# A quarter of the later weight splits made by GpSimd, and a planner with new prices

## The chip, the cores and the metric

The kernel runs on one core of a Trainium2 chip. The metric is the device time of one execution in microseconds, lower is better. A measured time is the median over runs; a profiled execution is one more run, with the hardware profiler on.

## The reference

One decoder layer on 512 tokens of width 2048, batch 1, in float32:

```python
mod = silu(c) @ w_ada + b_ada                  # six vectors of 2048: sh1 sc1 g1 sh2 sc2 g2
h   = rms_norm(x, norm1_g) * (1 + sc1) + sh1
u   = h @ w_in                                 # columns: conv b, c, h | q | 3 branches of k, v | gates
y_conv = u_b * causal_conv3(u_c * u_h)
k_cmp, v_cmp = compress(k), compress(v)        # gelu MLP over 31 overlapping blocks of 32 tokens
y_attn = g0 * compressed + g1 * selected + g2 * window attention   # 8 heads of 128, 2 kv heads
x   = x + g1 * ([rms_norm(y_conv) | rms_norm(y_attn)] @ w_out)
h   = rms_norm(x, norm2_g) * (1 + sc2) + sh2
x   = x + g2 * (relu(h @ w_ff1) ** 2 @ w_ff2)  # inner width 8192
out = rms_norm(x, normf_g)
```

## The kernel before, in words

**Precision.** Every large product of float32 matrices is made of three matmuls in the type fp32r. Each operand is split into a high part (ScalarE copies it into fp32r) and a low part (the operand minus its high part, a subtraction on VectorE). `mm3` issues high by high, high by low and low by high into one PSUM bank. So each block of weights needs a DMA, a copy on ScalarE and a subtraction on VectorE before its last third of matmuls can run.

**`weights(src)`** does that for the blocks of the layer's first part: 128 x 1024 (or 128 x 1072) float32, a DMA on the SP queue into a ring of three (`wraw`, tile `raw`), the ScalarE copy into `wh`, the VectorE subtraction into `wl`. `wh` and `wl` lie side by side in one tile, which the profile calls `wh` for both; there are two such tiles (`whl`), so a block's copy waits until the block two before it has been used up. Blocks of the compression weights take other buffers (tile `sw`, `spare=True`). `weights` is called 122 times: 16 `w_kv` and 16 `w_cv` blocks alternate in six stretches, then 32 of `w_conv` with 16 compression blocks between them, 8 of `w_v`, 16 of `w_q`, 16 of `w_oc` and 2 of `w_oa`. A block of the first two kinds is used by 24 matmuls of 512 columns.

**Other work on VectorE.** The conditioning `mod` is 192 dot products of a 128 x 1024 block of `w_ada` with `cs` (a `scalar_tensor_tensor` with an accumulator, tile `t<-wa,cs` in the profile), spread over the first part as a filler; 128 of them (`todo`) aren't needed until the attention. Rotary embeddings (`rope`, tile `rt`), the convolution (`vz`, `y`), the compression inputs (`ct`, `chi`, `clo`) and the softmax work run on VectorE too.

**Stages.** The first planned part (projections, convolution, compression) ends near 560 us of the profile. The second, attention with the out-projection of the convolution half (`out_conv`, tile `pw`) between its steps, ends near 747 us. The third holds the rest of the out-projection and the feed-forward part; it has its own splits (`hilo`, tile `hl`), which the change doesn't touch.

**The order of the work.** Nothing runs in the order of the Python text. An `Order` object stands in for the engines: it records each call with a cost (`price`, in us) and a lag, and `emit` makes a list schedule from them (`plan`) and issues the instructions in its order. The order on each engine is then fixed; on the chip the engines only wait for each other. The three planned parts have an `Order` each. The first two plan six times and keep the plan with the shortest planned time; the third plans once. Among the works that could begin at the same time, an engine takes the one with the earliest latest start (`late`), which is worked out backwards from planned TensorE times. GpSimd issues no instruction in the first two planned parts; in the third it issues DMAs.

Of the kernel before, what the change touches and what calls it, by code (L numbers as in the profile page):

```python
# [9 lines left out]
F32 = mybir.dt.float32  # L10
# [3 lines left out]
OP = mybir.AluOpType  # L14
AX = mybir.AxisListType

P = 128
# [18 lines left out]
NMAIN = 29  # L36
# [13 lines left out]
class Order:  # L50
# [8 lines left out]
        __slots__ = ("i", "eng", "call", "cost", "lag", "size", "preds", "succs", "late", "loose", "born",  # L59
                     "begin", "ready", "left", "lane", "slack", "due")  # L60

    def __init__(self, tc, tag, count, passes=1):
        self.tc, self.tag, self.count, self.passes = tc, tag, count, passes
        self.lane, self.kept, self.slack, self.wide = 0, set(), 0.0, (0.11, 0.00182)
        self.nodes, self.past, self.seen, self.rings = [], {}, {}, {}
        self.outer, self.loose, self.due = set(), False, 0.0
        for e in ("tensor", "vector", "scalar", "sync", "gpsimd"):
            setattr(self, e, Order.Engine(self, e, getattr(tc.nc, e)))
# [25 lines left out]
    def price(self, eng, op, out, ins, kw):  # L94

        n = Order.width(out)
        if "dma" in op:
            return (0.42 if eng == "sync" else 0.55), 0.0
        if eng == "tensor":
            if op == "matmul" and ins[0].dtype == F32:  # L100
                return max(self.wide[0], n * self.wide[1]), 0.2
            return (0.109 if op == "transpose" else max(0.1, 0.0015 + n * 0.000453)), 0.2
        if eng == "scalar":
            aps = len(ins) - 1
            more = 0.1 if kw.get("accum_out") is not None else 0.0
            return (0.18 if n < 16 else 0.09 + 0.00084 * n + (0.09 * max(0, aps) if not more else 0.19)), 0.16
        if op == "tensor_reduce":
            rows = max(Order.width(x) for x in ins)
            return 0.068 + 0.00104 * rows * (1.7 if n > 16 else 1), 0.14
        if n < 16:  # L110
            return 0.1, 0.14
        if op == "scalar_tensor_tensor":
            return 0.14 + 0.00101 * n, 0.14
        if op in ("tensor_scalar", "tensor_copy", "memset"):
            return 0.13 + 0.0005 * n, 0.14
        return 0.068 + 0.00104 * n, 0.14

    def record(self, eng, op, real, args, kw):
        is_ap = lambda x: hasattr(x, "dep_tracking_offset")
# [158 lines left out]
def hybrid_layer(ctx: ExitStack, tc: tile.TileContext, a, out):  # L278
    nc = tc.nc
# [10 lines left out]
    def slot(dtype=F32, name="m"):  # L290
        return mainp.tile([P, SLOT], dtype, name=name, tag="m")

    def pair(dtype=F32, name="m"):
        return slot(dtype, name)[:, :2 * T].rearrange("p (a b) -> p a b", a=2)
# [22 lines left out]
        tc.keep_in_program_order(filler(nc.tensor))  # L317

    xs = [pair(name="x2") for _ in range(NK // 2)]
    nc = order = Order(tc, xs[0].tensor.tag, NMAIN, passes=6)  # L320
    order.wide = (0.24, 0.0021)
    ts = [small.tile([P, T], F32, name="t", tag="t", bufs=5) for _ in range(5)]
    scr, temps = ts[0].bitcast(BF16), cycle(ts[1:])
# [18 lines left out]
    class lane:  # L342

        def __init__(self, n):
            self.n = n
# [15 lines left out]
    class floating:  # L361
# [4 lines left out]
        def __exit__(self, *_):  # L366
            order.loose = False

    def weights(src, cols=1024, spare=False):
        raw = next(wraw)[:, :cols]  # L370
        nc.sync.dma_start(out=raw, in_=src)
        wh, wl = (slot(F32R, name="sw") for _ in range(2)) if spare else next(whl)
        wh, wl = wh[:, :cols], wl[:, :cols]
        nc.scalar.activation(wh, raw, AF.Copy)
        nc.vector.tensor_tensor(out=wl, in0=raw, in1=wh.bitcast(F32), op=OP.subtract)
        return wh, wl

    def split(dst, src):
# [241 lines left out]
    def blob(s):  # L620
        return weights(a[steps[s][0]][steps[s][1]])
# [14 lines left out]
    for c in ada_steps(M_SH1 * NK):  # L636
        pass
    w = weights(a["w_kv"][0])
    low(*tokens(0, spread_r))
    order.slack = 1.0  # L640
# [8 lines left out]
    for s, (name, k) in enumerate(steps[:-1]):  # L649
# [4 lines left out]
        wh, wl = w  # L654
# [78 lines left out]
    def project(src, tiles):  # L733
        ps = bank()
        for half in range(2):
            wh, wl = ahead.pop() if ahead else weights(src(half))
            for j in range(8):
                k = half * 8 + j
                s = slice(j * P, (j + 1) * P)
                mm3(ps, wh[:, s], wl[:, s], tiles[k][:, 0], tiles[k][:, 1], k == 0, k == NK - 1)  # L740
            tick()
            more_ada(1)
        return ps
# [78 lines left out]
    for j in range(8):  # L822
# [4 lines left out]
        for i in range(3):  # L827
            n = 3 * j + i
# [30 lines left out]
    for g in range(NG):  # L859
        pv = [bank() for _ in range(NQ)]  # L860
        for blk in range(4):
            wh, wl = weights(a["w_v"][g * 4 + blk], BLOB)
# [11 lines left out]
        for t in range(NQ):  # L874
            if t % 2 == 0:
# [4 lines left out]
                                    in1=vv[g, t][:, 0].bitcast(F32), op=OP.subtract)  # L880
# [31 lines left out]
    for g in range(NG):  # L912
        pq = [bank() for _ in range(NR)]
        order_k = range(NK) if g < NG - 1 else range(NK - 1, -1, -1)
        for at, k in enumerate(order_k):
            if at % 2 == 0:
                wh, wl = weights(a["w_q"][g * 8 + k // 2])
# [32 lines left out]
    x1 = []  # L950
    nc = tc.nc
    temps = cycle(ts)
    nc = order = Order(tc, mix[0].tensor.tag, NMAIN, passes=6)
# [145 lines left out]
    front.close()  # L1099


    nc = order = Order(tc, x1[0].tensor.tag, NMAIN)
    ffn = ExitStack()
    ffp = ffn.enter_context(tc.tile_pool(name="ffp", bufs=2, reuse_waits="tile"))
    psf = ffn.enter_context(tc.tile_pool(name="psf", bufs=8, space=PSUM, reuse_waits="tile"))
# [32 lines left out]
    def raw_blob(src):  # L1138
        raw = next(rw)
        nc.sync.dma_start(out=raw, in_=src)  # L1140
        return raw

    def hl_tile(moved=False):
        t, o = next(hl), place[0] * SHIFT
        return t[:, o:o + 1024], Low(t, 1024 + o, moved)

    def hilo(dst, src, minus=False):
        high, low = dst
        nc.scalar.activation(high, src, AF.Copy, scale=-1.0 if minus else 1.0)
        for c in low.parts() if isinstance(low, Low) else [slice(0, 1024)]:  # L1150
            x, h = src[:, c], high[:, c].bitcast(F32)
            if minus:
                nc.vector.scalar_tensor_tensor(out=low[:, c], in0=x, scalar=-1.0, in1=h,
                                               op0=OP.mult, op1=OP.subtract)
            else:
                nc.vector.tensor_tensor(out=low[:, c], in0=x, in1=h, op=OP.subtract)
        return dst
# [20 lines left out]
    for k in range(8):  # L1178
        wh, wl = oa[k] if k < 2 else hilo(hl_tile(), raw_blob(a["w_oa"][k]))
# [254 lines left out]
    x1 = []  # L1434
# [60 lines left out]
    for f in range(8):  # L1495
# [7 lines left out]
        for q in range(3 if last else 4):  # L1503
            raw = [raw_blob(a["w_f2"][4 * f + q, b]) for b in range(4)]
# [127 lines left out]
```

## Time and profile before

| | |
|---|---|
| median of 3 runs | 2099.41 us (2098.15 to 2101.2) |
| profiled execution, its own time | 2105.6 us |
| its span, first to last instruction | 2103.8 us |
| mean granted TensorE clock | 0.989 |
| PE busy | 2060.6 us (98%), 15006 matmuls |
| DVE (VectorE) busy | 1886.2 us (90%) |
| ACT (ScalarE) busy | 1009.8 us (48%) |
| POOL (GpSimd) busy | 128.2 us (6%) |
| read from and written to HBM | 383.53 MB, 68.16 MB |

Nearly all instructions carry one source line, that of the planner's call, so work is told apart by its tiles: `ps` and `pw` are PSUM tiles of the first two parts, `pf` those of the third; `wh<-raw` is a copy into a high part, `wh<-raw,wh` the subtraction into a low one. Rows of a timeline begin with the start and the duration in us; brackets hold the idle time in front of the instruction on its engine and what ended it.

### The profile page before, as it was taken

The numbers are of one execution on the slowest core, as the hardware profiler recorded it, in microseconds if no ns is written. First come the engines' busy times: TensorE is split into PE (matmuls) and PEld (weight loads), VectorE is DVE, ScalarE is ACT, GpSimd is POOL, SyncE is SP. The second block draws the span as 40 slices with busy tenths as digits, with TensorE's granted clock in tenths as the row PEclk, the third lists the DMA queues.
The fourth block names the chain that finished last, engine by engine and source line by source line (L and its number), as shares of the span: only waits on it lengthen the run. The fifth ranks groups of instructions, "written<-read, shape, count | busy, mean of one in ns | idle before, by whom it ended". The sixth has DMA issues, their size and how long they took to land.

```text
span 2103.8 us, 38070 instructions
## 1 busy us (share of the span) xinstructions
PE 2060.6 (98%) x15006; PEld 1918.9 (91%) x15006; DVE 1886.2 (90%) x3104; ACT 1009.8 (48%) x1469; POOL 128.2 (6%) x244
## 2 busy tenths in 40 slices
PE   8999999999999999999999999999999999999997
PEld 6888787898888779999999999999999999999996
DVE  7998987887998647999999999999899999999997
ACT  5432333232455435766666666666433333333354
POOL 0000000000000001021122112211000000000000
PEclk8999999999999999999999999999999999999998
DMA  8996488888521244376676667669876466466442
GB/s 331 342 341 246 160 299 320 310 306 293 187 91 41 71 140 161 121 236 211 205 217 202 204 205 219 205 203 305 302 277 220 150 244 240 144 235 247 153 163 90
DMA packets 144274, 454.17 MB, mean 216 GB/s; under 512 B 15840, under 2 KB 20320, under 8 KB 144096
## 3 DMA queue, kind: packets, MB, share of 16 engines
q1 hardware_dynamic: 108960, 386.72, 52.8%
q0 software_dynamic: 34048, 63.98, 9.7%
q8 instruction: 118, 1.93, 0.4%
q10 hardware_dynamic: 1088, 1.05, 0.1%
q14 instruction: 60, 0.49, 0.1%
HBM read 383.53 MB, written 68.16 MB: 215 GB/s over the span
## 4 chain that ended last, share of the span: by engine, by line
PE 76%; DVE 7%; DMA 3%; ACT 2%; issue 1%; DVEq 0%; ACTq 0%; SPq 0%
PE pf L124 56%; PE ps L124 11%; PE pw L124 4%; PE pv L124 2%; PE s L124 2%; DVE t L124 1%; DVE hl L124 1%; PE pt L124 1%; DVE x L124 1%; DMA raw<-in_cmp_w 1%; DMA rw<-in_w_f 1%; DMA wa<-in_w_ada 1%; DMA tk<-g 1%; DVE tk L124 1%; DVE wh L124 1%
## 5 line engine op out<-in xcount | busy, mean ns | idle before, releaser
L124 PE MATMUL pf<-tk,hl 128*128 128x256 f32 x10704 | 1222.7, 277 | 3.4 <-DVE hl L124 3.1
L124 PEld LDWEIGHTS pf<-tk,hl 128*128 128x128 f32 x10704 | 1220.3, 188 | 4.7 <-DVE hl L124 3.5
L124 ACT ACTIVATE hl<-rw 128x1024 fp32r<-128x1024 f32 x269 | 285.6, 1062 | 332.6 <-PE pf L124 287.1
L124 DVE TENSOR_TENSOR hl<-rw,hl 128x1024 fp32r<-128x1024 f32 (+2 forms) x351 | 336.0, 967 | 30.7 <-ACT hl L124 30.5
L124 ACT ACTIVATE hl<-sg 128x1024 fp32r<-128x1024 f32 x180 | 191.2, 1063 | 221.9 <-PE pf L124 175.0
L124 DVE SCALAR_TENSOR_TENSOR t<-wa,cs 128x1024 bf16<-128x1024 f32 x192 | 234.2, 1220 | 25.4 <-DMA wa<-in_w_ada 23.1
L124 PE MATMUL ps<-h_m,wh 128*128 128x512 f32 x1080 | 252.4, 390 | 1.2 <-DVE wh L124 0.8
L124 PEld LDWEIGHTS ps<-h_m,wh 128*128 128x128 f32 x1080 | 201.1, 188 | 43.0 <-DVE wh L124 1.2
L124 ACT ACTIVATE wh<-raw 128x1024 fp32r<-128x1024 f32 (+1 forms) x106 | 112.6, 1062 | 251.1 <-PE ps L124 221.1
L124 DVE TENSOR_TENSOR hl<-sg,hl 128x1024 fp32r<-128x1024 f32 (+2 forms) x193 | 187.9, 985 | 28.1 <-ACT hl L124 28.1
L124 PE MATMUL ps<-h,wh 128*128 128x512 f32 x840 | 201.0, 395 | 3.7 <-ACT h L124 2.3
L124 PEld LDWEIGHTS ps<-h,wh 128*128 128x128 f32 x840 | 159.1, 191 | 38.4 <-ACT h L124 2.7
L124 DVE TENSOR_TENSOR sg<-sg,rw 128x1024 f32<-128x1024 f32 x120 | 145.9, 1216 | 0.2
L124 DVE SCALAR_TENSOR_TENSOR x<-pf,mod,x 128x256 f32<-128x256 f32 (+1 forms) x280 | 132.0, 484 | 15.6 <-PE pf L124 13.6
L124 DVE TENSOR_TENSOR wh<-raw,wh 128x1024 fp32r<-128x1024 f32 (+1 forms) x106 | 129.6, 1223 | 18.1 <-ACT wh L124 17.6
L124 POOL DMA_DIRECT2D g<-gt x192 | 101.2, 532 | 377.3 <-ACT hl L124 255.1
L124 PE MATMUL pw<-mix,wh 128*128 128x512 f32 x384 | 110.3, 409 | 0.0
L124 ACT ACTIVATE t<-t 128x512 f32<-128x512 f32 (+3 forms) x131 | 74.8, 571 | 18.6 <-DVE t L124 16.4
L124 DVE TENSOR_TENSOR sg<-rw 128x1024 f32<-128x1024 f32 x60 | 73.1, 1218 | 11.4 <-DMA rw<-in_w_f 6.7
L124 PEld LDWEIGHTS pw<-mix,wh 128*128 128x128 f32 x384 | 69.7, 192 | 11.1 <-issue 0.7
L124 DVE TENSOR_TENSOR rw<-rw 128x1024 f32<-128x1024 f32 x60 | 72.9, 1215 | 0.0
L124 ACT ACTIVATE gt<-t 128x512 fp32r<-128x512 f32 x96 | 60.4, 630 | 17.1 <-DVE t L124 13.9
(213 smaller groups left out, 1770.3 us busy)
## 6 DMA issues: line engine op xcount, KB each, us to landing
rw<-in_w_f SPq DMA_DIRECT2D x263, 512.0 KB, 4.0
wa<-in_w_ada SPq DMA_DIRECT2D x192, 512.0 KB, 6.2
tk<-g SPq DMA_DIRECT2D x114, 512.0 KB, 6.2
g<-gt POOLq DMA_DIRECT2D x192, 256.0 KB, 4.1
raw<-in_w_conv SPq DMA_DIRECT2D x32, 512.0 KB, 4.2
x<-in_xt SPq DMA_DIRECT2D x16, 512.0 KB, 6.9
raw<-in_w_kv SPq DMA_DIRECT2D x16, 512.0 KB, 4.7
raw<-in_w_cv SPq DMA_DIRECT2D x16, 512.0 KB, 4.1
```

The lines of the kernel that those rows point to most:

```text
L124: x.i, x.eng, x.call = len(self.nodes), eng, (lambda: real(*args, **kw))
```

## The change

```diff
+    def __init__(self, tc, tag, count, passes=1, pace=0.000456):
 ...
     if eng == "tensor":
         ...
-        return (0.109 if op == "transpose" else max(0.1, 0.0015 + n * 0.000453)), 0.2
+        return (0.109 if op == "transpose" else max(0.1, n * self.pace)), 0.2
+    if eng == "gpsimd":
+        return 0.3 + 0.0021 * n, 0.2
 ...
     if n < 16:
-        return 0.1, 0.14
+        return 0.12, 0.14
     if op == "scalar_tensor_tensor":
-        return 0.14 + 0.00101 * n, 0.14
+        return 0.14 + 0.00101 * n + (0.07 if kw.get("accum_out") is not None else 0.0), 0.14
 ...
-    return 0.068 + 0.00104 * n, 0.14
+    return 0.068 + 0.00104 * n + (0.1 if op == "tensor_tensor_reduce" or out.shape[0] < P else 0.0), 0.14
 ...
-nc = order = Order(tc, xs[0].tensor.tag, NMAIN, passes=6)        # first part
+nc = order = Order(tc, xs[0].tensor.tag, NMAIN, passes=6, pace=0.000444)
 ...
+    blobs = [0]
     def weights(src, cols=1024, spare=False):
         ...
         nc.scalar.activation(wh, raw, AF.Copy)
-        nc.vector.tensor_tensor(out=wl, in0=raw, in1=wh.bitcast(F32), op=OP.subtract)
+        blobs[0] += 1
+        engine = nc.gpsimd if blobs[0] > 16 and blobs[0] % 4 == 0 else nc.vector
+        engine.tensor_tensor(out=wl, in0=raw, in1=wh.bitcast(F32), op=OP.subtract)
 ...
-nc = order = Order(tc, x1[0].tensor.tag, NMAIN)                  # third part
+nc = order = Order(tc, x1[0].tensor.tag, NMAIN, pace=0.000444)
```

Of the 122 blocks that `weights` makes, those with the numbers 20, 24, 28 and so on to 120 get their low half from GpSimd: 26 blocks. The compression's blocks have odd numbers from 39 to 73, so none of these is among them. The copies on ScalarE and the matmuls stay.

The planner's prices change in all three parts: a matmul of 512 columns goes from 0.2335 to 0.2273 us in the first and third part (0.2335 in the second), one of 256 columns from 0.1175 to 0.1137 us. On VectorE, operations on fewer than 16 elements, `scalar_tensor_tensor` with an accumulator, `tensor_tensor_reduce`, and operations on fewer than 128 partitions are priced higher. A GpSimd operation on 1024 elements is priced at 2.45 us. The orders on all engines are planned anew with these.

More of the change, by code (lines that the diff above doesn't have):

```diff
@@ L60 @@
                      "begin", "ready", "left", "lane", "slack", "due")
-    def __init__(self, tc, tag, count, passes=1):
+    def __init__(self, tc, tag, count, passes=1, pace=0.000456):
         self.tc, self.tag, self.count, self.passes = tc, tag, count, passes
-        self.lane, self.kept, self.slack, self.wide = 0, set(), 0.0, (0.11, 0.00182)
+        self.lane, self.kept, self.slack, self.wide, self.pace = 0, set(), 0.0, (0.11, 0.00182), pace
         self.nodes, self.past, self.seen, self.rings = [], {}, {}, {}
```

## The prediction

> **What bounds the kernel now.** I read the page first: the shares.
>
> ```profile
> span 2103.8 us, 38070 instructions
> PE 2060.6 (98%) x15006; PEld 1918.9 (91%) x15006; DVE 1886.2 (90%) x3104; ACT 1009.8 (48%) x1469; POOL 128.2 (6%) x244
> ```
>
> TensorE is busy 98% of the span, so an engine that is relieved helps only where TensorE waits for it. Busy time also hides a halved clock, so I next cut the span into stretches. The columns are the length, busy time and instruction count of PE, PEld, DVE, ACT and POOL, then the granted TensorE clock, DMA share and GB/s.
>
> ```profile
> 60.00:160.00 100.00, 100.00 (x443) 82.84 (x442) 98.36 (x179) 39.68 (x51) 0.00 (x0) 1.00 0.92 345
> 176.00:226.00 50.00, 49.38 (x216) 39.92 (x215) 46.31 (x69) 13.56 (x16) 0.00 (x0) 1.00 0.46 160
> 226.00:237.00 11.00, 6.71 (x29) 4.60 (x27) 11.00 (x15) 6.07 (x8) 0.00 (x0) 0.96 0.28 95
> 237.00:244.00 7.00, 7.00 (x24) 6.06 (x25) 6.93 (x10) 1.44 (x2) 0.00 (x0) 0.57 0.58 192
> 244.00:440.00 196.00, 193.84 (x1001) 161.44 (x1001) 163.91 (x241) 63.41 (x76) 0.00 (x0) 1.00 0.83 301
> 440.00:549.00 109.00, 108.47 (x592) 94.94 (x591) 90.64 (x146) 34.37 (x53) 0.00 (x0) 1.00 0.78 283
> 549.00:562.00 13.00, 11.51 (x57) 9.36 (x55) 12.39 (x26) 3.60 (x6) 0.00 (x0) 1.00 0.72 250
> 562.00:572.00 10.00, 9.94 (x42) 8.44 (x43) 7.48 (x36) 5.07 (x20) 0.00 (x0) 0.66 0.42 150
> 572.00:730.00 158.00, 158.00 (x832) 126.53 (x831) 129.91 (x373) 86.35 (x219) 0.00 (x0) 1.00 0.18 61
> 900.00:1450.00 550.00, 550.00 (x4847) 550.00 (x4846) 520.44 (x747) 355.49 (x497) 108.83 (x207) 1.00 0.69 212
> 1500.00:1520.00 20.00, 17.27 (x134) 16.88 (x133) 16.96 (x30) 6.01 (x8) 2.63 (x5) 0.91 0.96 316
> 1530.00:2050.00 520.00, 520.00 (x4583) 520.00 (x4582) 500.88 (x740) 209.96 (x209) 0.58 (x2) 1.00 0.59 207
> ```
>
> From 60 to 160 us VectorE is 98% busy and TensorE still never waits: 443 matmuls of 512 columns in 100 us, 0.2257 us each. The feed-forward stretches run at 550/4847 = 0.1135 us per matmul of 256 columns. There nothing is to be gained. What VectorE can give back lies in two places. From 226 to 237 us VectorE is busy all 11.0 us and TensorE idles 11.0 - 6.71 = 4.3 us; the clock is then 0.57 for 7 us, another 7 x 0.43 = 3.0 us. At the seam to the attention, 549 to 562 us, it idles 1.5 us and then runs at 0.66 for 10 us, 3.4 us more. Which waits these are, the order in time shows (start, length, and in brackets the idle time before and who ended it):
>
> ```profile
> 227.63 4.19 PE L124 MATMUL ps<-h_m,wh 128*128 128x512 f32 x17 [0.82 <-DVE wh L124]
> 232.39 0.33 PE L124 MATMUL ps<-sw,chi 128*66 128x256 f32 x1 [0.57 <-ACT sw L124]
> 236.97 0.48 PE L124 MATMUL ps<-sw,chi 128*66 128x256 f32 x1 [2.89 <-DVE sw L124]
> 220.44 1.06 ACT L124 ACTIVATE wh<-raw 128x1024 fp32r<-128x1024 f32 x1 [0.15 <-ACT vz L124]
> 226.37 1.21 DVE L124 TENSOR_TENSOR wh<-raw,wh 128x1024 fp32r<-128x1024 f32 x1
> 231.30 1.04 ACT L124 ACTIVATE sw<-raw 128x1024 fp32r<-128x1024 f32 x1
> 235.71 1.21 DVE L124 TENSOR_TENSOR sw<-raw,sw 128x1024 fp32r<-128x1024 f32 x1
> ```
>
> The two VectorE waits, 0.82 and 2.89 us, are subtractions that stood in VectorE's queue: the `wh` one could have begun at 221.5 and began at 226.37, the `sw` one could at 232.3 and began at 235.71.
>
> **The change part by part.** *Blocks off VectorE.* The durations per piece:
>
> ```profile
> L124 DVE TENSOR_TENSOR wh<-raw,wh 128x1024 fp32r<-128x1024 f32 (+1 forms) x106 | 129.6, 1223 | 18.1 <-ACT wh L124 17.6
> L124 ACT ACTIVATE wh<-raw 128x1024 fp32r<-128x1024 f32 (+1 forms) x106 | 112.6, 1062 | 251.1 <-PE ps L124 221.1 <-issue 13.0 <-PE pw L124 7.0
> ```
>
> 26 x 1.223 = 31.8 us leave VectorE. Counting the `wh<-raw,wh` subtractions in order of time and skipping the compression's numbers, block 28 is the one at 177.8, 32 at 202.4, and 36 is the row at 226.37 above. So three lie in the full stretch before the long wait, 3 x 1.21 = 3.6 us, against 2.89 us of wait for `sw`; and block 36 itself is the 0.82 us wait. GpSimd has nothing else up to 730 us (POOL 0.00 in every row).
>
> *What GpSimd costs.* No GpSimd arithmetic is in this trace. The nearest row is VectorE's own 1.22 us, the lower end; the upper end that matters is where TensorE would notice: a block's 24 matmuls take 24 x 0.2257 = 5.4 us, the copy takes 1.06 of them, so 4.3 us. I take the planner's price from the diff, 2.45 us, near the middle. Then copy and subtraction are 3.5 of 5.4 us: the matmuls of the block before hide it, and the cost is nothing for 25 blocks. Block 36 would be ready at 221.5 + 2.45 = 224.0, before the 226.4 at which VectorE now begins it. The Trainium skill, GPSIMD Reference, section Elementwise — side-by-side cycle accounting, gives 4497 ns for 2048 elements of this operation, from which 2.25 us is an estimate for 1024; no run here shows it yet, and the sum would stay the same.
>
> (a) So of 0.82 + 2.89 + 3.0 = 6.7 us nearly all could go. But the next compression block is behind a transfer:
>
> ```profile
> 243.41 1.06 ACT L124 ACTIVATE sw<-raw 128x1024 fp32r<-128x1024 f32 x1 [5.56 <-DMA raw<-in_cmp_w]
> ```
>
> A TensorE that is earlier meets that one earlier. I take -5.0; ends -6.7 and +2.
>
> (b) Seam. Four blocks of `w_q` (92 to 104) leave VectorE, 4.9 us, but its last dot product waited for its transfer, and TensorE's wait was for what comes behind it:
>
> ```profile
> 559.20 1.23 DVE L124 SCALAR_TENSOR_TENSOR t<-wa,cs 128x1024 bf16<-128x1024 f32 x1 [0.40 <-DMA wa<-in_w_ada]
> 561.98 0.56 PE L124 MATMUL s<-kslc,q 128*128 128x160 f32 x3 [1.49 <-DVE pc L124]
> ```
>
> I take -1.0; ends -4.9 (wait and slow clock gone) and +1.
>
> (c) Block 120 lies where the attention ends, on the chain that set the end:
>
> ```profile
> 734.42 1.06 ACT L124 ACTIVATE wh<-raw 128x1024 fp32r<-128x1024 f32 x1 [0.79 <-PE pw L124]
> 735.51 1.23 DVE L124 TENSOR_TENSOR wh<-raw,wh 128x1024 fp32r<-128x1024 f32 x1
> 736.66 5.38 DVE L124 SCALAR_TENSOR_TENSOR ya<-ya,vec,sacc 128x512 f32<-128x512 f32 x8
> 735.96 0.60 ACT L124 ACTIVATE sacc<-pt 128x512 f32<-128x512 f32 x1 [0.48 <-PE pt L124]
> 749.36 10.73 PE L124 MATMUL pf<-mixa,wh 128*128 128x512 f32 x46 [1.00 <-DVE wh L124]
> ```
>
> VectorE gains nothing: `ya` needs `sacc`, which ends at 736.56 anyway. TensorE gets its low half at 735.5 + 2.45 = 737.9 instead of 736.7, 1.2 us later, with little else to do. I take +1.0; ends 0 and +1.3. Block 116 and the two before it sit amid attention work that fills TensorE (158.00 of 158.00 us).
>
> (d) *Prices.* The old plan has matmuls of 512 columns at 0.2335 us, the chip 0.2257, the new plan 0.2273; for 256 columns 0.1175, 0.1135, 0.1137. VectorE was too cheap:
>
> ```profile
> L124 DVE SCALAR_TENSOR_TENSOR t<-wa,cs 128x1024 bf16<-128x1024 f32 x192 | 234.2, 1220 | 25.4 <-DMA wa<-in_w_ada 23.1
> L124 DVE TENSOR_TENSOR rt<-part,rot 64x512 f32<-64x512 f32 (+1 forms) x18 | 11.8, 684 | 0.2
> ```
>
> The dots go from 1.174 to 1.244 (chip 1.220), the half-height rotary steps from 0.600 to 0.700 (chip 0.684). The old plan thus had TensorE 3% late and VectorE early, which is how (a) could go unseen in it; its repair is counted there. No instruction is added. But all orders are redrawn. From 244 to 549 us TensorE idles only 2.2 + 0.5 = 2.7 us; a redrawn order can lose there as well as win: +0.5, ends -2.7 and +4. In the feed-forward the one stretch with a loss is 1500 to 1520 us, 2.7 us idle and 20 x 0.09 = 1.8 us of clock: 0, ends -3 and +3.
>
> Sum: -5.0 - 1.0 + 1.0 + 0.5 = -4.5 us. Each duration is from the profiled execution, 2105.6 us (span 2103.8 and 1.8 around it), 6.2 us over the median of the runs; I set the difference against the median: 2099.4 - 4.5 = 2094.9 us.
>
> **The rivals.** *The stall only moves.* The first wait shrinks, but the transfer for the next compression block (the row at 243.41) or the redrawn order puts another in its place, and a gap of a few us anywhere brings the slow clock back, as behind both waits above. Then (a) is worth 2 instead of 5: 2099.4 - 2.0 - 1.0 + 1.0 + 0.5 = 2097.9 us. For it speaks that the 5.56 us of that row are a transfer, which no engine's relief shortens; against it, that its buffer is freed by the engines that now run earlier.
>
> *VectorE is held while GpSimd reads (slower).* If an instruction of VectorE with two inputs in SBUF cannot run beside one of GpSimd, each block costs VectorE up to 2.45 us of standing still for 1.22 saved, a net +1.2. It decides as soon as VectorE is held more than 1.2 us per block. Between 176 and 226 us VectorE has 3.7 us idle, enough for block 28; blocks 32 and 36 add 2.5 us ahead of `sw`, so that (a) turns into about +2 (2.5 more, 0.8 less, and the slow clock stays). The 17 blocks from 244 to 549 us add 17 x 1.2 = 21 us to VectorE, which has 196.0 - 163.9 + 109.0 - 90.6 = 50 us idle there; at 0.2 us each on TensorE, +3.5. At block 120 `ya` starts at 737.9 in place of 736.7: +1.3 more. Together 2.0 + 3.5 + 1.0 + 1.3 = +7.8: 2107.2 us. Nearly all VectorE work in that stretch (dots, subtractions) has two SBUF inputs, which speaks for its size; that no GpSimd arithmetic is in the trace leaves it open. The Trainium skill states this rule, in SBUF — State Buffer, section Who interferes with whom: a VectorE instruction with two SBUF inputs and a GpSimd instruction that reads SBUF exclude each other, and the second to issue blocks until the first is done. By that rule the sum would be the +7.8 just worked out; no row here can show it, since POOL computes nothing in these stretches.
>
> *GpSimd is slower than 4.3 us.* Then TensorE waits in 22 blocks; at 5 us it would be 22 x 0.7 = 15 us: 2110 us. Nothing in the trace speaks for it; it counts with the slower cases.
>
> **How the numbers follow.** About 0.2%, 4.2 us, is what a measurement can tell from no change: the borders are 2095.2 and 2103.6. The forecast's case, 0.42, with a range of its own from 2088 to 2095; the stall that moves, with small net changes of both signs, 0.35; slower, 0.23 (held 0.2, slow GpSimd 0.03). The held case does not get more, since part of VectorE's standing still falls into its idle time. Low end of the range: (a) -6.7, (b) -4.9 and (c) 0 give 2087.8, so 2087. High end: the held case, 2107. That leaves about 0.2 outside.
>
> **What would show it.** Right: 26 subtractions on POOL of about 2.5 us, VectorE's count of `wh<-raw,wh` down to 80, the wait for `sw` near 230 us under 1 us and no stretch at half clock behind it. Held: VectorE's subtractions and dots beside a POOL instruction take 2 to 3.5 us instead of 1.22. Moved: the same idle sum of TensorE before 560 us under other names. Wrong altogether: the feed-forward, planned once with new prices, changes by more than 3 us; there (e.g. at 1500 us) I count nothing.

## The result, and the profile after

The changed kernel takes 2114.8 us (median of 6 runs, 2113.6 to 2122.4), the one before 2099.4 in the same session: a ratio of 1.0083, 95% interval 1.0067 to 1.0099. It is slower by 15 us by the medians and 17 by the ratio, where 2094.9 us was forecast and the range ended at 2107. The ratios here and below are those on record with their intervals, and differ somewhat from the quotients of the medians (here 1.0073); the median given with each is its own.

The page of the changed kernel, shares:

```profile
span 2113.7 us, 38138 instructions
PE 2057.6 (97%) x15006; PEld 1919.3 (91%) x15006; DVE 1891.1 (89%) x3078; ACT 1007.7 (48%) x1469; POOL 195.7 (9%) x270
```

VectorE has 26 instructions fewer (3078 against 3104), which took 31.8 us, and yet 1891.1 us of busy time in place of 1886.2. So the others grew by 36.7 us (1891.1 less 1886.2 - 31.8). The groups show GpSimd's work, and dot products that were 1220 ns each and are now 1268 in the mean, with 41.8 us of idle time in front of them instead of 25.4:

```profile
L126 POOL TENSOR_TENSOR wh<-raw,wh 128x1024 fp32r<-128x1024 f32 (+1 forms) x26 | 67.5, 2597 | 686.3 <-ACT wh L126 458.1 <-DVE aff L126 131.0 <-PE pw L126 49.1
L126 DVE SCALAR_TENSOR_TENSOR t<-wa,cs 128x1024 bf16<-128x1024 f32 x192 | 243.4, 1268 | 41.8 <-DMA wa<-in_w_ada 39.8
```

Where the time of VectorE went is seen beside each GpSimd subtraction. In order of time, three of them with VectorE's instructions next to them (start, length):

```profile
131.40 3.41 POOL L126 TENSOR_TENSOR wh<-raw,wh 128x1024 fp32r<-128x1024 f32 x1 [130.96 <-DVE aff L126]
131.33 1.22 DVE L126 SCALAR_TENSOR_TENSOR t<-wa,cs 128x1024 bf16<-128x1024 f32 x1
132.49 2.34 DVE L126 SCALAR_TENSOR_TENSOR mod<-acc,vec 128x1 f32<-128x1 f32 x1
...
310.76 3.26 POOL L126 TENSOR_TENSOR wh<-raw,wh 128x1024 fp32r<-128x1024 f32 x1 [18.63 <-ACT wh L126]
311.69 2.87 DVE L126 TENSOR_TENSOR sacc<-sacc,t 128x512 f32<-128x512 f32 x1
...
657.95 2.40 POOL L126 TENSOR_TENSOR wh<-raw,wh 128x1024 fp32r<-128x1024 f32 x1 [48.11 <-PE pt L126]
658.27 0.28 DVE L126 CUSTOM_DVE_ANT_0 p<-s,causal 128x128 f32<-128x128 f32 x1
658.86 0.69 DVE L126 TENSOR_TENSOR tt<-pt,tt 128x512 fp32r<-128x512 f32 x1 [0.30 <-ACT tt L126]
```

No row names the hold as a wait; it is read from the lengths. At 131.4 GpSimd's row begins, 3.41 us long where an undisturbed one takes 2.40, so it first waits for the dot product that VectorE is in, until about 132.5. Then it runs, and VectorE's next instruction, one element wide, stands until 134.8, when GpSimd is done. `sacc<-sacc,t`, 0.68 us before, takes 2.87 and ends 0.5 us behind GpSimd. At 658 VectorE reads its first operand from PSUM, and nothing is held: 0.28 and 0.69 us are these groups' usual times. The instructions beside all 26 subtractions are together 35.0 us longer than instructions of the same kind and shape are without GpSimd (in `e3`): 10.6 us beside the first five, 21.5 beside the 17 from block 40 to 104, 2.8 beside the four in the attention. Each block saves VectorE 1.22 us, so the first five cost it 4.5 us net and the 17 only 0.8.

What TensorE makes of it (the two long waits, then stretches with the columns as before):

```profile
235.28 0.48 PE L126 MATMUL ps<-sw,chi 128*66 128x256 f32 x1 [5.64 <-ACT sw L126]
576.24 0.93 PE L126 MATMUL s<-kslc,q 128*128 128x160 f32 x3 [9.00 <-DVE pc L126]
```

```profile
226.00:240.00 14.00, 8.36 (x31) 6.53 (x30) 14.00 (x19) 7.45 (x9) 0.00 (x0) 0.78 0.23 67
240.00:440.00 200.00, 192.20 (x978) 159.77 (x977) 161.15 (x222) 63.06 (x75) 28.68 (x11) 1.00 0.81 290
564.00:576.00 12.00, 2.48 (x15) 1.66 (x13) 9.96 (x23) 1.07 (x2) 0.00 (x0) 0.68 0.80 273
576.00:586.00 10.00, 9.76 (x38) 9.00 (x39) 5.41 (x36) 5.25 (x20) 0.00 (x0) 0.53 0.24 95
```

The wait near 230 us did not shrink, it grew from 4.3 us of idle time in all to 5.6. It carries another name now, ScalarE's `sw`, but it is still VectorE's queue: ScalarE makes `sw` behind its copy into `chi`, and that one stood for VectorE's `ct`.

```profile
233.22 1.06 ACT L126 ACTIVATE chi<-ct 128x1024 fp32r<-128x1024 f32 x1 [3.62 <-DVE ct L126]
```

From 240 to 440 us TensorE idles 7.8 us, where it was 2.2 in 244 to 440. The seam to the attention, 1.5 us before, is 9.5 us idle in one stretch, with the clock at 0.53 for 10 us behind it. The last dot product, behind which the attention's first work stands, starts at 573.5 instead of 559.2 (rows of the dots, shortest, median and longest in ns, then first and last start, before and after):

```profile
L124 DVE SCALAR_TENSOR_TENSOR t<-wa,cs x192: 1161/1219/1243, 16.6 to 559.2; 128x1024 bf16<-128x1024 f32 x192
```

```profile
L126 DVE SCALAR_TENSOR_TENSOR t<-wa,cs x192: 1202/1220/3302, 16.3 to 573.5; 128x1024 bf16<-128x1024 f32 x192
```

The third part got shorter. From its first matmul to the end, before and after; and the stretch that had the one loss before:

```profile
747.70:2103.80 1356.10, 1333.25 (x11448) 1320.94 (x11448) 1242.20 (x1890) 711.54 (x960) 128.02 (x240) 0.99 0.62 205
```

```profile
765.00:2113.70 1348.70, 1330.12 (x11448) 1319.04 (x11448) 1241.88 (x1890) 709.08 (x960) 127.92 (x240) 1.00 0.63 207
1500.00:1520.00 20.00, 19.76 (x173) 19.55 (x172) 18.81 (x30) 8.87 (x12) 0.00 (x0) 1.00 0.80 296
```

So the loss of the first two parts is about 17 us in these two profiles, and 7.4 us came back in the third.

### The profile page after: what moved, and what is told of

Same layout as the page of the kernel before. It is cut to its first block, busy times and chain, and to the rows that moved or that the text cites. A ratio compares the mean times of both kernels' runs of the same rounds, so it can differ in the third digit from the quotient of the medians.

```text
span 2113.7 us, 38138 instructions
## 1 busy us (share of the span) xinstructions
PE 2057.6 (97%) x15006; PEld 1919.3 (91%) x15006; DVE 1891.1 (89%) x3078; ACT 1007.7 (48%) x1469; POOL 195.7 (9%) x270
## 4 chain that ended last, share of the span: by engine, by line
PE 85%; DVE 8%; DMA 4%; issue 2%; ACT 1%; SPq 0%; DVEq 0%; ACTq 0%
PE pf L126 61%; PE ps L126 16%; PE pw L126 4%; DMA wa<-in_w_ada 2%; DVE t L126 2%; PE pv L126 2%; PE s L126 2%; DVE wh L126 1%; PE pt L126 1%; DVE rt L126 1%; DMA raw<-in_cmp_w 1%; DMA tk<-g 1%; DMA rw<-in_w_f 1%; DVE x L126 0%; DVE vz L126 0%
## 5 line engine op out<-in xcount | busy, mean ns | idle before, releaser
L126 DVE SCALAR_TENSOR_TENSOR t<-wa,cs 128x1024 bf16<-128x1024 f32 x192 | 243.4, 1268 | 41.8 <-DMA wa<-in_w_ada 39.8
L126 POOL TENSOR_TENSOR wh<-raw,wh 128x1024 fp32r<-128x1024 f32 (+1 forms) x26 | 67.5, 2597 | 686.3 <-ACT wh L126 458.1
L126 DVE TENSOR_TENSOR wh<-raw,wh 128x1024 fp32r<-128x1024 f32 (+1 forms) x80 | 97.9, 1224 | 12.4 <-ACT wh L126 11.8
L126 DVE TENSOR_TENSOR sg<-rw 128x1024 f32<-128x1024 f32 x60 | 73.1, 1218 | 11.4 <-DMA rw<-in_w_f 9.2
```

The source lines that it names most:

```text
L126: x.i, x.eng, x.call = len(self.nodes), eng, (lambda: real(*args, **kw))
```

## The experiments

The theories: **H**, VectorE is held while GpSimd reads, and that costs the time; **P**, the new prices draw worse orders; **L**, GpSimd's low half comes later than VectorE's; and on how a hold reaches TensorE, **D** (through the late dot products at the seam) and **Q** (through waits before it). All ratios are to the kernel before; edits are shown shortened. A new order of the instructions is drawn for every version, and the first two parts keep the old one only in `e3`.

**1. New prices alone.** `e1_prices_only`:

```diff
-engine = nc.gpsimd if blobs[0] > 16 and blobs[0] % 4 == 0 else nc.vector
+engine = nc.vector
```

> All new prices, but VectorE makes every low half, as before the change. Theory H (held): VectorE instructions with two SBUF inputs stand still while GpSimd reads, at moments the plan does not know of, and that is what costs TensorE the time before the third part; then without GpSimd the third part begins near 748 us as before (746 to 751) and the total is the changed kernel's third part on top of it, 2092 to 2097 us. Theory P (prices): the new prices by themselves draw a worse order for the first two parts, and holding costs only the net 35.0 - 31.8 = 3 us of VectorE; then the third part begins at 760 us or later and the total is 2109 to 2114 us.

Measured: 0.9998 (0.9982 to 1.0015), median 2100.3 us. Neither: the 15 us are gone without GpSimd, but the third part's gain is not visible in the sum either, so the new prices by themselves cost the first two parts about what they bring the third. Its third part begins at 746.6 us, as theory H had it, but the total is above H's range. The profile shows both sides. From 226 to 240 us TensorE idles only 1.6 us at full clock, so the new order does repair the stall that the prediction put under (a). At the seam, with no GpSimd at all, TensorE arrives at 548.5 us, ten earlier than before, and waits 11.65 us, longer than in the changed kernel.

```profile
226.00:240.00 14.00, 12.39 (x61) 10.01 (x60) 13.97 (x19) 6.83 (x10) 0.00 (x0) 1.00 0.33 105
563.02 0.93 PE L126 MATMUL s<-kslc,q 128*128 128x160 f32 x3 [11.65 <-DVE pc L126]
```

**2. GpSimd alone.** `e2_gpsimd_old_prices` keeps the 26 subtractions and GpSimd's price; every other price is the old one:

```diff
-nc = order = Order(..., passes=6, pace=0.000444)    # and likewise in the other two parts
+nc = order = Order(..., passes=6, pace=0.000444, new=False)
```

> The 26 low halves on GpSimd, at the planner's 2.45 us each, but all other prices as before the change, in all three parts. Theory H: the first two parts lose as in the changed kernel, the third gains nothing: 2112 to 2124 us, with VectorE instructions stretched by 30 to 40 us in sum. Theory P: about the net 3 us of VectorE: 2099 to 2104 us.

Measured: 1.0106 (1.0082 to 1.0130), 2121.7 us. Theory H: GpSimd costs 22 us by itself (17 to 27 by the interval), the order drawn anew for it included. VectorE has 26 instructions fewer, and is busy 1892.9 us in this profile, 38.5 more than 1886.2 - 31.8. TensorE doesn't wait at the seam here: its last work ahead of it ends at 574.4 us, and the last dot product starts at 572.8. The loss is in waits ahead of it.

**3. New prices in the third part alone.** `e3_third_part`: no GpSimd, `new=False` in the first two parts, so their orders are those of the kernel before.

> No GpSimd; the first two parts keep the old prices, the third part alone is planned with the new ones. If the third part's 7 us (1348.6 us in the changed kernel, 1356.1 before) are the new prices' doing, this gives 2099.4 - 7 = 2092 us (2089 to 2095) under both theories. If they come from how the third part is entered, it stays at 2099 (2096 to 2102).

Measured: 0.9964 (0.9951 to 0.9978), 2092.0 us. The 7.6 us are the new prices' doing in the third part. This version beats both kernels. Its third part:

```profile
737.60:2084.70 1347.10, 1328.39 (x11448) 1317.50 (x11448) 1241.80 (x1890) 709.46 (x960) 127.89 (x240) 1.00 0.62 207
```

It also warns about single profiles: the first two parts, in the same order, end at 737.6 us here and at 747.7 in the profile before. Most of that is the slow clock: here TensorE waits 2.85 us for the same `sw` subtraction and 0.86 at the seam (at 555.0), and neither stretch behind is slow.

```profile
234.54 0.33 PE L126 MATMUL ps<-sw,chi 128*66 128x256 f32 x1 [2.85 <-DVE sw L126]
237.00:244.00 7.00, 6.36 (x29) 4.96 (x28) 6.90 (x12) 2.30 (x3) 0.00 (x0) 1.00 0.48 160
552.00:562.00 10.00, 9.10 (x57) 7.38 (x56) 9.58 (x45) 5.91 (x20) 0.00 (x0) 1.00 0.60 221
```

So single differences under 10 us between profiles, those of the section above too, say where time went and not how much the change costs; that is read from the medians and ratios.

**4. A plan that knows of the hold.** `e4_plan_knows`, in `plan`:

```diff
+if e == "gpsimd" and not x.size: at = max(at, free["vector"])
 ...
 free[e] = at + x.cost
+if e == "gpsimd" and not x.size: free["vector"] = at + x.cost
```

> The changed kernel, but the planner books VectorE too for the 2.45 us of each GpSimd subtraction and starts it only where VectorE is free. Theory H, with the surprise as the cost: the orders fit the chip again, and most of the loss returns although VectorE still loses 26 x 1.2 = 32 us net: 2096 to 2104 us. Theory H, with the lost VectorE time itself as the cost: 2108 to 2116. Theory P: still 2109 to 2116.

Measured: 1.0092 (1.0063 to 1.0120), 2118.3 us. Above all three ranges: in sum, knowing of it gains nothing. In this profile the first part's matmuls end at 550 us, 14 earlier than in the changed kernel's, and the seam takes it all back: the last dot starts at 575.8 us and TensorE waits 14.11 us for what comes behind it. So the plan could take the waits ahead of the seam away, but not the time that VectorE loses.

```profile
L126 DVE SCALAR_TENSOR_TENSOR t<-wa,cs x192: 1154/1219/3395, 17.2 to 575.8; 128x1024 bf16<-128x1024 f32 x192
578.62 0.93 PE L126 MATMUL s<-kslc,q 128*128 128x160 f32 x3 [14.11 <-DVE pc L126]
```

**5. Only the attention's four blocks.** `e5_attention_four` is `e3` with

```diff
+engine = nc.gpsimd if blobs[0] > 104 and blobs[0] % 4 == 0 else nc.vector
```

> The kernel of e3 (old prices in the first two parts, new ones in the third, 2092 us), with GpSimd making only the four blocks 108, 112, 116 and 120 of the attention part. There VectorE reads PSUM for much of its work, and in the changed kernel two of the four subtractions held nothing, two held 1.6 and 1.2 us, against 4 x 1.22 saved. Theory H: no loss, 2089 to 2095 us. If any block on GpSimd costs its share of the whole loss (22 us for 26, 0.8 each), 2095 to 2098.

Measured: 0.9963 (0.9946 to 0.9980), 2095.2 us; `e3` had 0.9964 and 2092.0 us. By the ratios the four cost nothing and bring nothing; the interval leaves room for 0.8 us each, and the median lies on the border of the two expectations. It decides little.

**6. Twice as many.** `e6_every_second` is the changed kernel with `blobs[0] % 2 == 0`.

> The changed kernel with every second block on GpSimd in place of every fourth: 53 in place of 26. Theory H with the lost VectorE time as the cost: holding doubles to about 70 us, and what GpSimd costs against the prices alone (2114.8 - 2100.3 = 14.5 us) doubles: 2124 to 2135 us. If the loss comes from a few badly placed blocks and not from the sum, it stays near the changed kernel: 2110 to 2120.

Measured: 1.0087 (1.0065 to 1.0109), median 2122.2 us; the changed kernel has 1.0083. Over the new prices alone (`e1`) GpSimd costs 0.89% here and 0.85% there; twice that, 1.7%, lies outside the interval, so the expected doubling failed. By the medians it is somewhat more, 22.6 us over the kernel before in place of 15.4. The hold did double: VectorE has 53 instructions fewer (64.8 us) and is busy 1897.6 us, 76.2 more than that leaves, in place of 36.7. The time does not follow the sum of the holds. Theory L has a part here: TensorE waits 1.8 us for one of GpSimd's low halves.

**7 and 8. Fewer dot products at the seam.** Both leave out the last 16 of the 192 dot products with their transfers and set these columns to zero, `e7_fewer_dots` in the changed kernel, `e8_before_fewer_dots` in the one before:

```diff
 m = todo.pop(0)
 acc = halves_of(m)
+if m >= M_G2 * NK + 8:
+    for i in range(2):
+        nc.vector.memset(acc[i], 0.0)
+    bias_in(m, acc)
+    continue
```

> The changed kernel, but the last 16 of the 192 dot products of w_ada (eight columns of g2) are left out with their transfers and set to zero. Theory D: what VectorE loses is paid at the seam to the attention, where the late dot products stand in front of the attention's first work; without the last 16 (16 x 1.27 = 20 us of VectorE) the 9.0 us wait there goes with the slow clock behind it (3 to 4 us): 2100 to 2105 us. Theory Q: the loss is TensorE's many waits for low halves before the seam; they stay, and with it 2110 to 2115 us.

> The kernel before the change, with the same 16 dot products left out. Theory D: only the small wait at the seam is there to win, 1.5 us and 3.4 us of slow clock: 2094 to 2098 us; the difference to the run of the changed kernel without them is then under 8 us, of which the third part takes 8 back, where it was 15. Theory Q: 2097 to 2100 us.

Measured: 1.0006 (0.9993 to 1.0020), 2103.1 us, and 0.9975 (0.9955 to 0.9994), 2096.9 us. The changed kernel gains 0.77%, the one before 0.25%. Both times lie in theory D's ranges. The wait at the seam is gone in the changed kernel (last dot at 543.5 us):

```profile
L126 DVE SCALAR_TENSOR_TENSOR t<-wa,cs x176: 1159/1220/3507, 17.6 to 543.5; 128x1024 bf16<-128x1024 f32 x176
564.31 0.46 PE L126 MATMUL s<-kslc,q 128*128 128x160 f32 x3
```

By the ratios the changed kernel is 0.83% behind (17.4 us), and 7.6 us more that the third part gave back: 25 in the first two parts. Without the late dots it is 0.31% (6.5 us) and 7.6: 14. So about 11 us of the loss (0.52%; 9 by the medians, uncertain by some 6) go with the late dots, and about 14 stay, in waits before the seam or in the attention: D and Q both. That the 11 us are the hold's doing is not shown: `e1`, with nothing held, waits even longer at the seam.

**9 and 10. The hold by itself.** `e9_extra_read` is `e3`, VectorE making every low half, plus a subtraction on GpSimd whose result nobody reads; `e10_extra_write` writes at the same places and reads nothing:

```diff
 nc.vector.tensor_tensor(out=wl, in0=raw, in1=wh.bitcast(F32), op=OP.subtract)
+if blobs[0] > 16 and blobs[0] % 4 == 0:
+    nc.gpsimd.tensor_tensor(out=raw, in0=raw, in1=wh.bitcast(F32), op=OP.subtract)   # e9
+    nc.gpsimd.memset(raw, 0.0); nc.gpsimd.memset(raw, 0.0)                           # e10
```

> The kernel of e3 (2092 us): VectorE makes every low half. Behind it GpSimd does the same subtraction once more for blocks 20, 24, ... 120, into the raw tile, whose value nobody reads after that; its next use waits for GpSimd. So nothing is taken off VectorE, and no matmul waits for GpSimd's result. Theory H (held): VectorE is stretched by 25 to 40 us in sum, now with nothing saved, and the time is 2108 to 2130 us. Theory L (late): what cost TensorE in the changed kernel is that GpSimd's low half comes 1.2 us later than VectorE's; here nobody waits for it, so 2092 to 2097 us.

> As e9, but GpSimd fills the raw tile with zeros twice in place of the subtraction: it writes as often or more and reads nothing, with the same waits around it. If only GpSimd's reading holds VectorE, no VectorE instruction is stretched and the time is that of e3, 2090 to 2096 us. If its writing holds too, or if the later return of the raw tile is what costs, the time is like e9's.

Measured: 1.0131 (1.0105 to 1.0157), 2122.7 us, and 1.0002 (0.9992 to 1.0012), 2098.4 us. The pages of the two, `e9` first:

```profile
PE 2062.6 (97%) x15006; PEld 1917.9 (90%) x15006; DVE 1924.7 (91%) x3104; ACT 1008.8 (48%) x1469; POOL 202.4 (10%) x270
L126 POOL TENSOR_TENSOR raw<-raw,wh 128x1024 f32<-128x1024 f32 (+1 forms) x26 | 74.3, 2856 | 686.2 <-DVE wh L126 511.8 <-DMA wa<-in_w_ada 174.3
```

```profile
PE 2055.7 (98%) x15006; PEld 1916.7 (91%) x15006; DVE 1886.3 (90%) x3104; ACT 1008.4 (48%) x1469; POOL 178.0 (8%) x296
L126 POOL MEMSET raw<- 128x1024 f32 (+1 forms) x52 | 49.9, 960 | 688.7 <-DVE wh L126 687.2
```

With the same 3104 instructions VectorE is busy 38.4 us longer beside a GpSimd that reads, and not at all beside one that only writes. Between the two lie 1.29%, 27 us (21 to 33); nobody waits for the low half here, so theory L can't account for it. The two differ in a little more than the reading: the planner prices one subtraction at 2.45 us and two fills at 4.9, so the orders are alike but not the same, and the raw tile comes back after 2.9 us in the mean or 1.9. What TensorE waited for from 60 to 545 us shows that these count for less: 21.6 us in all in `e9` and 6.4 in `e10`, and of the 15 us between them 2.1 are under ScalarE's `sw`, the rest under tiles that VectorE makes (`e9` first, then `e10`; total, number, longest).

```profile
PE ps L126 <- DVE sw L126: 6.9, 6, 2.1
PE ps L126 <- ACT sw L126: 6.0, 5, 2.8
PE ps L126 <- DVE part L126: 2.4, 2, 1.8
PE ps L126 <- DVE t L126: 2.2, 1, 2.2
```

```profile
PE ps L126 <- ACT sw L126: 3.9, 3, 3.1
PE ps L126 <- DVE wh L126: 1.1, 2, 0.8
```

`e10` itself is 0.38% (8 us) over `e3`, more than expected: the raw tile comes back later, and the orders were drawn anew; which of the two, was not tried.

**11 and 12. Which blocks.** `e11_middle_blocks` is `e3` with blocks 40 to 104 on GpSimd, `e12_first_five` with 20 to 36:

```diff
+engine = nc.gpsimd if 40 <= blobs[0] <= 104 and blobs[0] % 4 == 0 else nc.vector   # e11
+engine = nc.gpsimd if 20 <= blobs[0] <= 36 and blobs[0] % 4 == 0 else nc.vector    # e12
```

> The kernel of e3 with GpSimd making the 17 blocks 40 to 104 only: not the five that fall where VectorE is full (20 to 36), not the four in the attention. If the loss of the first two parts (22 us over e3) follows the number of held blocks, 17 of 22 give 2092 + 17 = 2109 us (2105 to 2113). If it is made in the full stretch (176 to 245 us) by blocks 28 to 36, little is left: 2092 to 2099 us.

> The kernel of e3 (0.9964 of the time before) with GpSimd making only the five blocks 20 to 36, the ones in and ahead of the stretch where VectorE is full. All 26 blocks cost 22 us (e2), the 17 of the middle 0.46% or 10 us (e11 over e3), the four in the attention nothing (e5). If these add up, five blocks cost 12 us: 1.002 of the time before, 2104 us (1.000 to 1.004). If holds cost by their number, five of 26 cost 4 us: 0.9984, 2096 us (0.997 to 0.9995).

Measured: 1.0010 (0.9998 to 1.0021), 2099.5 us, and 0.9992 (0.9981 to 1.0003), 2097.1 us. Over `e3` the 17 blocks cost 0.46%, 10 us, or 0.6 each; the five 0.28%, 6 us, or 1.2 each; the four of the attention nothing. Each of these is uncertain by 4 us, and `e10` shows that a new order with nothing held can cost 8. So neither a price per block nor a ranking of places is shown, nor whether the three, 16 us together, fall short of the 22. `e11` lies between its two expectations, `e12` in the range of the second. And `e12` is not a pure hold: VectorE's instructions followed one another without a gap, GpSimd's row for the fifth block is 7.17 us long, of which some 4.8 are waiting, and TensorE waits 3.36 us for its low half. Theory L, of no weight in the changed kernel, is right there.

```profile
227.48 7.17 POOL L126 TENSOR_TENSOR wh<-raw,wh 128x1024 fp32r<-128x1024 f32 x1 [25.51 <-ACT wh L126]
232.40 2.79 DVE L126 SCALAR_TENSOR_TENSOR vz<-vz,vec 128x511 f32<-128x511 f32 x1
234.70 2.79 PE L126 MATMUL ps<-h_m,wh 128*128 128x512 f32 x11 [3.36 <-POOL wh L126]
```

**The runs side by side.** The stretch from 60 to 545 us, ahead of the seam, in the profiles of before, the changed kernel, `e1`, `e2`, `e4`, `e9` and `e10`, in this order:

```profile
60.00:545.00 485.00, 477.40 (x2350) 399.71 (x2349) 426.94 (x667) 160.69 (x205) 0.00 (x0) 0.99 0.79 289
60.00:545.00 485.00, 468.96 (x2316) 393.75 (x2315) 421.62 (x628) 155.01 (x196) 55.05 (x21) 0.99 0.78 281
60.00:545.00 485.00, 482.21 (x2396) 406.83 (x2395) 428.87 (x668) 163.88 (x207) 0.00 (x0) 1.00 0.80 290
60.00:545.00 485.00, 464.91 (x2280) 386.79 (x2279) 417.77 (x626) 152.23 (x191) 56.36 (x21) 0.99 0.78 284
60.00:545.00 485.00, 480.69 (x2386) 404.86 (x2385) 420.49 (x620) 158.92 (x201) 59.10 (x22) 1.00 0.77 278
60.00:545.00 485.00, 463.42 (x2269) 386.58 (x2268) 439.71 (x641) 152.03 (x190) 58.22 (x20) 0.99 0.78 280
60.00:545.00 485.00, 478.58 (x2374) 402.37 (x2373) 429.69 (x670) 162.38 (x206) 40.28 (x42) 1.00 0.79 290
```

TensorE idles 7.6, 2.8 and 6.4 us where nothing is held, and 16.0, 20.1 and 21.6 where VectorE is held and the plan doesn't know. The others fit: 7.1 in `e5` and 7.4 in `e8`, which hold nothing here, and 13.7 in `e7`, 15.9 in `e11`, 15.4 in `e12` and 21.2 in `e6`. Five held blocks (`e12`) idle TensorE as long as 26, so the loss doesn't go by their number. With a plan that knows (`e4`) it is 4.3, and the loss stands at the seam. VectorE has 45 to 67 us idle in this stretch in all of them. So the loss ahead of the seam is less a lack of VectorE time than results that come late.

## Why the prediction was wrong

**The step that failed is "the cost is nothing for 25 blocks".** The sum let 31.8 us leave VectorE and charged nothing for GpSimd working beside it. The runs showed that VectorE stands while GpSimd reads: its other instructions grew by 36.7 us, more than was saved, a GpSimd that reads cost 27 us against one that only writes (`e9`, `e10`), and the 26 blocks alone cost 22 us (`e2`). So what (a) and (b) counted on did not come.

**The ranking of the rivals.** The prediction had the held VectorE as a rival at 0.2, and its condition, more than 1.2 us per block, came true: 1.35 in the mean. The reason for giving it no more was that part of the standing still falls into idle time; that bears on what a hold costs, not on whether it happens. No row of the trace before spoke against it. The Trainium skill, SBUF — State Buffer, section Who interferes with whom, states the rule, and the trace agrees with the parts that the rows above show: two SBUF inputs held (0.68 us became 2.87), an operand from PSUM not held (0.69 us), a GpSimd that only writes not holding (1886.3 us busy).

**The price of a hold at TensorE, 0.2 us per block.** The rival's sum, +7.8, was worked out from it, and 2107.2 us fell short of 2114.8. Measured are 22 us for 26 blocks (`e2`), 0.8 each, and 10 us for the 17 that the 0.2 was meant for (`e11`), 0.6 each, a new order included. The reasoning was that VectorE has 50 us idle from 244 to 549 us, of which the 17 blocks would take 21. They took 0.8 net, and yet TensorE waited: what counted was not how full VectorE was, but which of its results came late, those for the compression's `sw` above all. From 60 to 545 us TensorE's waits under `sw`, ScalarE's and VectorE's together, are 12.0 us in the changed kernel, 11.4 in `e2` and 12.9 in `e9`; where nothing is held they are 5.1 (before), 2.0 (`e1`) and 3.9 (`e10`). The idle time before the dots, 25.4 us before and 41.8 after, doesn't measure it: it is 21.7 in `e9`, where VectorE is held as long.

**(a), -5.0.** Wrong in sign. Blocks 28, 32 and 36 took 3.6 us off VectorE, and the instructions beside them took 3.30, 2.78 and 2.88 us in place of 1.22, 0.69 and 0.74: 6.3 us of standing still. TensorE's idle time there went from 4.3 to 5.6 us, and the slow clock stayed. The 3.0 us of slow clock in (a), like the 3.4 in (b), were a matter of that one profiled execution: `e3`, in the same order, waits as long for `sw` and runs at full clock behind it. So they could not be counted as won against the median, and a gap of a few us does not always bring the slow clock.

**(b), the seam, -1.0, worst case +1.** It became the largest single wait, 9.0 us, and 9 to 11 us of the loss go with the late dots (`e7`, `e8`). The step saw that TensorE waited for what comes behind the last dot, and did not ask when the dots would end in a new order. `e1` waits 11.65 us there with nothing on GpSimd, `e2` not at all. So the long wait at the seam comes with the new prices, and what the hold does to it is to let both sides come later: TensorE arrives at 564.5 us in place of 548.5 in `e1`, and the last dot starts at 573.5 in place of 560.3.

**(c), block 120, +1.0.** Not separable; with the other three of the attention it came to nothing that can be told from noise (`e5`).

**(d), prices.** The repair of (a) did come from them (`e1`, 1.6 us idle near 230 us), but the redrawn order as a whole was sized at +0.5 for 244 to 549 us and nothing for the seam. In the first two parts the new prices cost about 0.34% (`e1` against `e3`), 7 us, uncertain by 5. The feed-forward was sized at 0, -3 to 3, and gained 7.6 us, which by the prediction's own last sign is "Wrong altogether": of that, 2.5 us of idle time and 1.8 us of clock lay in 1500 to 1520 us, the place that was named; the rest is spread over the part and was not traced. These two errors nearly cancel, which is luck; without the third part's gain the changed kernel would have been some 7 us slower still.

**What was right.** 26 subtractions at 2.6 us on POOL against 2.45 taken; alone, with nothing to wait for, one takes 2.4 (the row at 657.95), between the planner's 2.45 and the 2.25 estimated from the Trainium skill, GPSIMD Engine Reference. `wh<-raw,wh` on VectorE fell to 80. The sign for the held case, 2 to 3.5 us in place of 1.22, is what the dots show (up to 3.30). That the low half comes later costs nothing that the changed kernel's profile shows: none of TensorE's waits names POOL. It is not so in every order: `e12` and `e6` have such a wait, 3.36 and 1.8 us.

**Open.** Why twice as many blocks cost hardly more (`e6`), how much of each version's time is the hold and how much the order drawn for it (no run holds VectorE in an order that is otherwise the same), and when a wait of TensorE brings the slow clock and when not.

## What to carry to other kernels

An engine that seems idle may hold up the one to be relieved when both work: before work is moved, look at what the relieved engine will be executing beside it (here, how many operands it takes from SBUF), and price the moved instruction as time of both. Where the loss shows depends on the order: many small waits for late results (`e2`, `e9`), or one long one at the deadline of a filler stream like the dot products (`e4`). So look at which results come late and when the filler's last instruction runs, not at the mean load. And when a change mixes prices of a planner with a move of work, try the parts separately: the version that keeps only the new prices of the third part (0.9964) was inside a change that lost 0.8%.

## What was not expected of the hardware

- An instruction of one element per partition (`mod<-acc,vec`, 0.21 us) took 2.34 us beside GpSimd: it was held until GpSimd was done, like a long one.
- GpSimd is not let in after one instruction of VectorE in every case: in `e12` it stood some 4.8 us while VectorE ran six instructions without a gap between them, then ran its own 2.4.
- A `tensor_scalar` with one SBUF tensor input was held too, 2.04 us in place of 0.41 (the row before it with the same shape took 0.42), unlike the instructions with an operand in PSUM at 658 us:

```profile
607.44 2.39 POOL L126 TENSOR_TENSOR wh<-raw,wh 128x1024 fp32r<-128x1024 f32 x1 [49.07 <-PE pw L126]
608.01 2.04 DVE L126 TENSOR_SCALAR p<-p,cf 128x384 f32<-128x384 f32 x1
```

- The same instruction order of the first two parts ended 10 us apart in two profiled executions (737.6 and 747.7 us), with a wait of 2.9 us for the same `sw` in both and the slow clock behind it in one only.
